# Rotary embedding: moving the cos table's load from ScalarE's queue to SyncE's, behind the first piece of x

## The chip, the cores and the metric

One core of one Trainium2 chip. The metric is the device time of one execution in microseconds (us); lower is better. The engines are called TensorE (PE in the profile, PEld for its weight loads), VectorE (DVE), ScalarE (ACT), GpSimd (POOL) and SyncE (SP). SyncE computes nothing here; it issues DMAs.

## The reference

```python
# x: (16, 512, 1024) float32; cos, sin: (512, 32) float32; num_heads = 16
x = x.reshape(batch, seq, num_heads, head_dim)           # head_dim 64, half_dim 32
x1, x2 = x[..., :half_dim], x[..., half_dim:]
cos = cos[None, :, None, :]; sin = sin[None, :, None, :]
rotated = np.concatenate([x1 * cos - x2 * sin, x1 * sin + x2 * cos], axis=-1)
```

33.55 MB come in and 33.55 MB go out. The two tables are 64 KB each.

## The kernel before

x is cut into eight tiles of 4 MB (128 partitions, 8 rows of 1,024 elements on each). There are places for five tiles; a result overwrites its input and is stored from there. Everything that moves x is issued by SyncE, in a fixed order: five tiles in, stores 0, 1 and 2, load 5, load 6 and 7 together, and the remaining stores.

```python
FIRST = (3, 8)                       # tile 0 comes as rows 0-2, then rows 3-7
# ... (pools, helpers)
tabs = bp.tile([P, 2 * dim], FP32, name="b")
sin_sb = tabs[:PB, : KK * half]                      # 64 partitions x 256
cos_sb = tabs[:PB, dim : dim + KK * half]
nc.scalar.dma_start(out=sin_sb, in_=sin_v)
nc.scalar.dma_start(out=cos_sb, in_=cos_v)
for _ in range(2):
    nc.sync.nop(hint="pause")
load(0, 0, FIRST[0])
for lo, hi in zip(FIRST, FIRST[1:]):
    load(0, lo, hi)
load(1)
load(2)
load_two(3)
# ... (identity, zeroed PSUM)
nc.tensor.matmul(out=sin_t, lhsT=spread, rhs=sin_sb, start=True, stop=True)   # 64 -> 128 partitions
nc.tensor.matmul(out=cos_t, lhsT=spread, rhs=cos_sb, start=True, stop=True)
# ... (sin_k: a view of sin_t)
nc.vector.tensor_scalar_mul(out=sns[:, :, 0, :], in0=sin_k, scalar1=-1.0)     # GpSimd's table
nc.vector.tensor_copy(out=sns[:, :, 1, :], in_=sin_k)
# ... (own_t: a part of the PSUM tile of cos)
nc.vector.tensor_copy(out=own_t, in_=sns[:, ROW_OWN])
# ... (helpers)
def stores(t):
    if t == 4:
        store_two(3)
    elif t != 3:
        store(t)
    if t == 2:
        load(5)
        load_two(6)
```

Per tile GpSimd multiplies x (halves swapped) by sin into a buffer `b`. VectorE multiplies x by cos into PSUM and adds the two (`pair_sum`, the line L199). TensorE adds for the remaining rows, and ScalarE copies those out. So GpSimd needs sin, and VectorE needs cos for its first product and GpSimd's `b` for each sum.

## Time and profile before

| | before |
|---|---|
| time, median of 6 runs | 162.32 us (162.24 to 162.7) |
| span of the profiled run | 160.7 us |
| VectorE busy | 136.3 us (85%) |
| GpSimd busy | 127.1 us (79%) |
| moved by DMA | 67.25 MB, mean 419 GB/s |
| sin, cos: issue to landing | 6.5 us, 9.3 us |
| last store: issue, landing | 148.2 us, 159.8 us |

Two things are to be read apart. A busy share tells how full an engine is on average. A DMA "lands" when the last of its sixteen completion signals, one for each DMA engine, has arrived. The landing of the last store is what ends the program. The prediction shows the lines.

### The profile page before, as it was taken

What the parts mean: (1) busy time and instruction counts of PE and PEld (TensorE: products, weight loads), DVE (VectorE), ACT (ScalarE), POOL (GpSimd) and SP (SyncE); (2) the same over time, 40 slices, a digit from 0 to 9 for tenths busy, and PEclk for the clock granted to TensorE, in tenths of its full rate; (3) what the DMA queues carried; (4) which work ended last, traced back from release to release, by engine and by line L of the source; (5) the groups of instructions that cost most, each with busy time, mean ns of one, the idle gap of its engine ahead of it and who ended that gap; (6) DMA issues with size and microseconds to landing.
All of it is one profiled execution on the core that took longest, in us unless ns stands there. A gap on an engine that the chain in (4) does not pass through costs nothing.

```text
span 160.7 us, 433 instructions
## 1 busy us (share of the span) xinstructions
PE 57.2 (36%) x71; PEld 18.8 (12%) x71; DVE 136.3 (85%) x85; ACT 18.0 (11%) x25; POOL 127.1 (79%) x38
## 2 busy tenths in 40 slices
PE   3140825055503731191309250645047402922000
PEld 0110301021102210121003010211022101310000
DVE  1029999999999999999999999999999999998000
ACT  0000331003000301021100310031003010201000
POOL 1069999999999889988998899892999999960000
PEclk9999995558555765567555955585557655675555
DMA  5999999999999999999999999999999999999993
GB/s 168 411 431 458 408 473 424 392 449 465 392 449 449 408 392 506 408 392 498 410 400 465 441 400 441 465 392 432 473 400 416 489 400 416 473 408 408 392 506 147
DMA packets 2562, 67.25 MB, mean 419 GB/s; under 512 B 257, under 2 KB 385, under 8 KB 385
## 3 DMA queue, kind: packets, MB, share of 16 engines
q1 hardware_dynamic: 2400, 67.11, 97.6%
q10 hardware_dynamic: 160, 0.13, 0.2%
q14 instruction: 2, 0.01, 0.0%
HBM read 33.69 MB, written 33.55 MB: 418 GB/s over the span
## 4 chain that ended last, share of the span: by engine, by line
DVE 74%; issue 11%; DMA 6%; PE 1%; ACTq 0%; DVEq 0%
DVE x L199 34%; DVE pd L151 33%; DMA b<-in_cos_dram 6%; DVE pe_ps L151 5%; DVE own_ps L151 1%; PE tab L124 1%; ACTq L91 0%; DVE x L160 0%; DVE tab L129 0%; DVEq L199 0%
## 5 line engine op out<-in xcount | busy, mean ns | idle before, releaser
L175 POOL TENSOR_TENSOR b<-x,sns 128x2048 f32<-128x2048 f32 (+1 forms) x32 | 126.4, 3983 | 15.4 <-DVE sns L127 8.1
L199 DVE TENSOR_TENSOR x<-pd,b 128x2048 f32<-128x2048 f32 x24 | 54.9, 2288 | 0.9
L151 DVE TENSOR_TENSOR pd<-x,tab 128x2048 f32<-128x2048 f32 x24 | 55.0, 2292 | 0.2
L186 PE MATMUL own_ps<-x,ident 128*128 128x512 f32 x32 | 29.6, 1082 | 53.3 <-DVE x L160 48.3
L186 PE MATMUL pe_ps<-b,ident 128*128 128x512 f32 x32 | 25.1, 877 | 27.2 <-DVE pe_ps L151 27.2
L186 PEld LDWEIGHTS own_ps<-x,ident 128*128 128x128 f32 x32 | 9.4, 324 | 73.2 <-DVE x L160 59.3
L219 ACT COPY x<-own_ps 128x1024 f32<-128x1024 f32 x8 | 8.1, 1013 | 72.8 <-PE own_ps L186 72.8
L191 ACT COPY x<-pe_ps 128x512 f32<-128x512 f32 x16 | 9.4, 589 | 38.7 <-PE pe_ps L186 38.7
L186 PEld LDWEIGHTS pe_ps<-b,ident 128*128 128x128 f32 x32 | 8.2, 286 | 42.2 <-DVE pe_ps L151 33.9
L151 DVE TENSOR_TENSOR pe_ps<-x,tab 128x512 f32<-128x512 f32 x16 | 11.0, 687 | 0.0
L151 DVE TENSOR_TENSOR own_ps<-x,tab 128x1024 f32<-128x1024 f32 x8 | 9.8, 1224 | 0.0
L160 DVE TENSOR_TENSOR x<-x,tab 128x1024 f32<-128x1024 f32 x8 | 9.7, 1214 | 0.0
L126 DVE TENSOR_SCALAR sns<-pd 128x256 f32<-128x256 f32 x1 | 0.4, 425 | 7.0 <-PE pd L123 7.0
L219 ACT ACT_TABLE_LOAD x1 | 1.3, 1283 | 16.8 <-DVE x L160 16.8
L123 PE MATMUL pd<-b,spread 64*128 64x256 f32 x2 | 1.2, 696 | 4.7 <-DMA b<-in_sin_dram 4.7
L129 DVE COPY tab<-sns 128x64 f32<-128x64 f32 x1 | 0.2, 228 | 2.6 <-PE tab L124 2.6
L124 PE MATMUL tab<-b,spread 64*128 64x256 f32 x2 | 1.2, 708 | 2.1 <-DMA b<-in_cos_dram 2.1
L111 PE MATMUL own_ps<-zero 128*128 128x512 bf16 x2 | 1.0, 622 | 1.2 <-DVE zero L107 1.2
L123 PEld LDWEIGHTS pd<-b,spread 64*128 64x128 f32 x2 | 0.5, 306 | 5.6 <-issue 5.6
L107 DVE MEMSET zero<- 128x256 uint32 x1 | 0.3, 272 | 0.9 <-PEq L250 0.9
L124 PEld LDWEIGHTS tab<-b,spread 64*128 64x128 f32 x2 | 0.5, 310 | 2.9 <-DMA b<-in_cos_dram 2.9
L111 PE MATMUL pe_ps<-zero 128*128 128x512 bf16 x1 | 0.6, 634 | 0.0
(9 smaller groups left out, 1.8 us busy)
## 6 DMA issues: line engine op xcount, KB each, us to landing
out_dram<-x SPq DMA_DIRECT2D x6, 4096.0 KB, 21.4
x<-in_x_dram SPq DMA_DIRECT2D x2, 8192.0 KB, 39.5
x<-in_x_dram SPq DMA_DIRECT2D x3, 4096.0 KB, 27.2
out_dram<-x SPq DMA_DIRECT2D x1, 8192.0 KB, 32.6
x<-in_x_dram SPq DMA_DIRECT2D x1, 2560.0 KB, 12.4
x<-in_x_dram SPq DMA_DIRECT2D x1, 1536.0 KB, 6.6
b<-in_sin_dram ACTq DMA_DIRECT2D x1, 64.0 KB, 6.5
b<-in_cos_dram ACTq DMA_DIRECT2D x1, 64.0 KB, 9.3
```

Source lines behind the costliest of these rows:

```text
L107: nc.vector.memset(zero, 0.0)
L111: nc.tensor.matmul(out=ps, lhsT=zero[:, :P], rhs=zero, start=True, stop=True)
L123: nc.tensor.matmul(out=sin_t, lhsT=spread, rhs=sin_sb, start=True, stop=True)
L124: nc.tensor.matmul(out=cos_t, lhsT=spread, rhs=cos_sb, start=True, stop=True)
L126: nc.vector.tensor_scalar_mul(out=sns[:, :, 0, :], in0=sin_k, scalar1=-1.0)
L151: nc.vector.tensor_tensor(out=o, in0=i, in1=cb, op=ALU.mult)
L160: nc.vector.tensor_tensor(out=heads(r), in0=heads(r), in1=s, op=ALU.mult)
L175: nc.gpsimd.tensor_tensor(out=o, in0=i, in1=sb, op=ALU.mult)
L186: nc.tensor.matmul(out=ps, lhsT=ident, rhs=other, start=False, stop=True, skip_group_check=True)
L191: nc.scalar.copy(out=r, in_=pe_ps)
L199: nc.vector.tensor_tensor(out=r, in0=ps, in1=b, op=ALU.add)
L219: nc.scalar.copy(out=r0, in_=own_ps)
```

## The change

The intent: let VectorE start earlier by bringing cos sooner. cos now stands on SyncE's queue, right behind the first piece of x, instead of behind sin on ScalarE's queue. The two no-ops that held SyncE back go.

```diff
     nc.scalar.dma_start(out=sin_sb, in_=sin_v)
-    nc.scalar.dma_start(out=cos_sb, in_=cos_v)
-    for _ in range(2):
-        nc.sync.nop(hint="pause")
     load(0, 0, FIRST[0])
+    nc.sync.dma_start(out=cos_sb, in_=cos_v)
     for lo, hi in zip(FIRST, FIRST[1:]):
         load(0, lo, hi)
```

Two lines fewer: L199 of the kernel before is L197 of the changed one, L151 is L149, L175 is L173.

## The prediction

> **What bounds the kernel now.** I read the page first, for busy shares and for the forty slices of DMA.
>
> ```profile
> span 160.7 us, 433 instructions
> PE 57.2 (36%) x71; PEld 18.8 (12%) x71; DVE 136.3 (85%) x85; ACT 18.0 (11%) x25; POOL 127.1 (79%) x38
> ...
> DMA 5999999999999999999999999999999999999993
> ...
> DMA packets 2562, 67.25 MB, mean 419 GB/s; under 512 B 257, under 2 KB 385, under 8 KB 385
> ```
>
> DVE at 85% looks like the bound, but the DMA row has a 9 in every slice except the first and the last, and 67.25 MB has to move. Second, the chain of waits, in order of time, over the first 20 us:
>
> ```profile
> 0.73 0.54 ACTq L91
> ...
> 1.30 9.32 DMA b<-in_cos_dram
> ...
> 10.66 1.23 PE tab L124 x2
> ...
> 11.92 0.24 DVE tab L129
> ...
> 12.18 1.23 DVE own_ps L151
> ```
>
> This is what the change aims at: the 64 KB of cos take 9.32 us from issue to landing, and VectorE's first product (L151) stands behind them until 12.18 us. From there the chain is nearly all VectorE. But it ends with VectorE's last sum at 148.15 us, 12.5 us before the span's end, because the last store is no engine's busy work. So, third, stretches (engine columns, then granted clock, DMA share, GB/s):
>
> ```profile
> 2.00:4.00 2.00, 0.65 (x2) 0.00 (x0) 0.00 (x0) 0.00 (x0) 0.00 (x0) 1.00 0.83 289
> ...
> 16.00:148.00 132.00, 53.30 (x64) 17.56 (x64) 130.82 (x78) 18.01 (x25) 119.83 (x31) 0.62 1.00 433
> 148.00:158.00 10.00, 0.00 (x0) 0.00 (x0) 0.15 (x1) 0.00 (x0) 0.00 (x0) 0.50 0.99 423
> 158.00:160.70 2.70, 0.00 (x0) 0.00 (x0) 0.00 (x0) 0.00 (x0) 0.00 (x0) 0.50 0.03 12
> ```
>
> From 16 to 148 us VectorE and DMA are both full (130.82 of 132 us, and a share of 1.00), so busy shares alone do not decide. What decides is whether a queue stands in front of the DMA engines when a store is issued. Fourth, the last three stores, one at a time (issue line, then time from issue to landing):
>
> ```profile
> L83 SPq DMA_DIRECT2D out_dram<-x x1: 357/357/357, 115.2 to 115.2; - x1
> ...
> DMA to landing us min/median/max: 25.3/25.3/25.3
> ```
> ```profile
> L83 SPq DMA_DIRECT2D out_dram<-x x1: 344/344/344, 132.2 to 132.2; - x1
> ...
> DMA to landing us min/median/max: 18.0/18.0/18.0
> ```
> ```profile
> L83 SPq DMA_DIRECT2D out_dram<-x x1: 332/332/332, 148.2 to 148.2; - x1
> ...
> DMA to landing us min/median/max: 11.6/11.6/11.6
> ```
>
> They land at 115.2 + 25.3 = 140.5, 132.2 + 18.0 = 150.2 and 148.2 + 11.6 = 159.8 us: 9.7 us apart, though they are issued 16 to 17 us apart. 4,194,304 bytes in 9.7 us is 432 GB/s, the rate of the whole middle. The queue of waiting bytes shrinks (25.3, 18.0, 11.6) but is not empty at the last one: an idle path would need about 1.0 us from issue to first packet (0.83 to 1.83 us for the first x piece, in the packet records), 9.7 us of data and 0.3 us from the last packet (159.52) to the landing (159.84), 11.0 us together. So some 0.6 us of work still stood ahead of the last store. **DMA sets the end**, and VectorE misses being the bound by only about 0.6 us.
>
> **What the Trainium skill says.** "DMA: Bandwidth & Descriptors", section "Issuing engines are not separate DMA queues": DMAs of SyncE, ScalarE and GpSimd run on the same 16 engines and interleave. The trace agrees: queue 1 (x and out) and queue 10 (tables) are served in turn from 4.15 to 10.2 us. Same page, "Queues, rings and completion order": each engine goes round-robin over its rings, packet by packet. The trace shows it one row at a time: a 1,024-byte table row (0.046 us) after each x row, of 12,288 bytes (0.46 us) or 20,480 bytes (0.82 us). "Perfetto Trace Analysis", section "Roofline": one active core is bounded by its 16 DMA engines, about 435 GB/s in total. The trace agrees with 433. Same page, "DMA Instruction — HWDGE (DVE, Sync)": the profiled window of an issue leaves out the data movement. So an SP issue of 0.4 us must not be read as a transfer, and I use landings.
>
> **The change, part by part.**
>
> 1. Two no-ops off SyncE. Its records show them at 0.721 and 0.767, with the first x issue at 0.828. Removed, that issue starts near 0.72, **0.11 us earlier**. Nothing is ahead of it, so the first packet (1.83 us) moves with it, and with it all the traffic behind it. This lies on the path.
>
> 2. cos off ScalarE's queue. 64 rows over 16 engines are 4 rows on each, for either table. sin goes first on queue 10 and takes the turns beside the 12 KB rows; cos gets its turns beside the 20 KB rows of the second piece, which is why it lands at 1.30 + 9.32 = 10.62 against sin's 7.21 (0.73 + 6.5). Each cos row stretches an engine's cycle from about 0.767 us (20 KB alone) to 0.854 us, 0.087 for a row whose own record is 0.046. Behind the first piece on SyncE's queue, the 4 rows should cost 4 x 0.046 = 0.18 us instead of 4 x 0.087 = 0.35. **0.16 us of DMA time saved**, on the path; this half rests on my reading of packet spacing and could be zero.
>
> 3. cos lands early. The first piece lands at 0.83 + 6.6 = 7.4 us now; with 0.11 off and 0.18 for the cos rows I estimate 7.5, three microseconds earlier. sin still lands near 7.2 and its two matmul passes run from 7.35 to 8.54; cos follows on TensorE at about 8.57 instead of 10.66. Matmul start to first product was 12.18 - 10.66 = 1.52 us, so the first product starts near **10.1 us, 2.1 us earlier**. GpSimd waits for sin alone (start 9.41) and does not move.
>
> 4. One more issue on SyncE (about 0.5 us) delays the second piece's issue from 1.27 to about 1.7 us, while the engines are busy with the first piece until 6.6: hidden.
>
> What is part 3 worth at the end? The stores come 2.1 us earlier into a queue that is already full. Their order is fixed in the program, all on SyncE's queue, and no byte disappears. It even gets lost before: the load of tiles 6 and 7 is issued at 82.4 us and takes 29.1, landing at 111.44, and VectorE starts tile 6 with almost no slack:
>
> ```profile
> 111.58 6.83 POOL L175 TENSOR_TENSOR b<-x,sns 128x2048 f32<-128x2048 f32 x2 [3.16 <-DMA x<-in_x_dram]
> 111.71 1.23 DVE L151 TENSOR_TENSOR own_ps<-x,tab 128x1024 f32<-128x1024 f32 x1
> ```
>
> VectorE would be ready at about 109.6 and would stand until 111.2 or so. So its 2.1 us are swallowed there, and its last sum still ends near 148. Part 3 adds **0** to the total. Sum: 0.11 + 0.16 = 0.27 us. 162.38 - 0.27 = **162.1 us**.
>
> **The rivals.**
>
> *VectorE is the bound, and the head start reaches the end:* 162.38 - 2.1 = 160.2 us. For it: 85% busy, and the chain of waits. Against it: the three landings 9.7 us apart, and the wait at 111.4 us, which ends with a transfer. 4 in 100.
>
> *The tables come later or disturb the start:* without the no-ops the first x issue goes out with or before sin, and sin's rows could wait behind more 12 KB rows, 0.46 us each; on the shared descriptor path ScalarE's issue could be held by SyncE's 0.38 us. GpSimd and VectorE would start up to 1 us later than I think. But against 12.18 today there is room, so the end hardly notices. It would cost only the 0.27 us: 162.4.
>
> *The transfers are merely reordered:* part 2 saves nothing, and only the no-ops count: 162.3 us. This lies well within the range.
>
> *A deeper pull into VectorE:* it now runs closer behind GpSimd. The slack at the first sum falls from 16.65 - 13.38 = 3.3 us (GpSimd's first product ends near 13.4) to about 1.1; at the second sum to a few tenths. Here part of the 2.1 us can turn into a wait on GpSimd, but VectorE would have to end over 0.6 us later than now to move the end.
>
> **Range and chances.** The three timed runs before lie at 162.28 to 162.7. My candidates lie at 162.1 (chosen), 162.3 to 162.4 (if a small term fails) and 160.2 (the first rival). With that spread and a tenth or two for the clock of the runs, 8 in 10 is 161.6 to 162.6. 2% is 3.2 us, more than even the first rival gives: faster 0.01, slower 0.01, same 0.98.
>
> **What would show it.** Right: cos lands near 7.5 us and the first product starts near 10.1; the last stores still land 9.7 us apart, with the time to landing of those before the tile 6 load grown by about 2 us; the idle time of VectorE before tile 6's first product grows to between 1 and 2 us, ended by the transfer of x; the last sum ends near 148 and the last landing is 0.1 to 0.4 us earlier. Wrong: the last store issued 2 us earlier and landing 2 us earlier (DMA was not the bound); a share of DMA that falls in a middle slice (a gap I don't expect); or sin landing after 8.5 us, so that the order of the tables costs what it should give.

## The result, and the profile after

| | before | changed |
|---|---|---|
| time, median of 6 runs | 162.32 us (162.24 to 162.7) | 162.46 us (162.14 to 162.74) |
| first x packet | 1.83 us | 1.74 us |
| sin landed / cos landed | 7.21 / 10.62 us | 7.71 / 7.91 us |
| GpSimd's first product | 9.41 us | 9.91 us |
| VectorE's first product | 12.18 us | 10.20 us |
| VectorE's second sum of tile 0 | 21.84 us | 21.26 us |
| last store issued | 148.23 us | 147.96 us |
| last store landed | 159.84 us | 159.73 us |

The ratio is 1.0003, 95% interval 0.9987 to 1.0019. Nothing measurable came of it, though VectorE's first product comes 1.98 us earlier.

The table's lower rows show where most of the 1.98 us went, in three steps. Here is the changed kernel in order of time (start, duration, engine, line, operation; in brackets the idle time before and what ended it):

```profile
9.91 22.57 POOL L173 TENSOR_TENSOR b<-x,sns 128x2048 f32<-128x2048 f32 x6 [8.60 <-DVE sns L125]
...
10.20 1.23 DVE L149 TENSOR_TENSOR own_ps<-x,tab 128x1024 f32<-128x1024 f32 x1
...
21.26 2.29 DVE L197 TENSOR_TENSOR x<-pd,b 128x2048 f32<-128x2048 f32 x1 [1.51 <-POOL b L173]
```
```profile
111.44 1.23 DVE L149 TENSOR_TENSOR own_ps<-x,tab 128x1024 f32<-128x1024 f32 x1 [0.22 <-DMA x<-in_x_dram]
111.48 6.83 POOL L173 TENSOR_TENSOR b<-x,sns 128x2048 f32<-128x2048 f32 x2 [3.65 <-DMA x<-in_x_dram]
```

And the lines of the kernel before that answer to the second sum and to the last store:

```profile
21.84 2.29 DVE L199 TENSOR_TENSOR x<-pd,b 128x2048 f32<-128x2048 f32 x1
```
```profile
148.23 0.33 SPq L83 DMA_DIRECT2D out_dram<-x  x1
```

First, VectorE waits 1.51 us for GpSimd at its second sum, a wait that the kernel before has not. GpSimd itself starts 0.50 us later than before, because sin lands 0.50 us later. But that is the smaller part. In the kernel before, GpSimd's product for this sum ended at 20.71 us by its own record (the next one began at 20.66), 1.13 us before VectorE's sum began. A head start of 1.98 us uses these up and runs 0.85 us ahead of GpSimd even with sin on time. Of 1.98 us, 21.84 - 21.26 = 0.58 are left, so 1.40 us are lost here.

Second, VectorE runs into the load of tiles 6 and 7 at 111.44 us; after it 111.71 - 111.44 = 0.27 us are left, which is what the last store's issue shows. The chain that ended last, followed back, now passes through two transfers here, the store of tile 2 and the load into the place that it frees; in the kernel before it stays on VectorE from 12.18 us on:

```profile
63.70 18.49 DMA out_dram<-x
...
82.27 29.08 DMA x<-in_x_dram
...
111.44 0.06 DVE own_ps L149
```

Third, the stores of the changed kernel wait in the same queue. The last three again, issue and time to landing:

```profile
L83 SPq DMA_DIRECT2D out_dram<-x x1: 357/357/357, 114.9 to 114.9; - x1
...
DMA to landing us min/median/max: 25.4/25.4/25.4
```
```profile
L83 SPq DMA_DIRECT2D out_dram<-x x1: 344/344/344, 131.9 to 131.9; - x1
...
DMA to landing us min/median/max: 18.2/18.2/18.2
```
```profile
L83 SPq DMA_DIRECT2D out_dram<-x x1: 333/333/333, 148.0 to 148.0; - x1
...
DMA to landing us min/median/max: 11.8/11.8/11.8
```

They land at 140.4, 150.1 and 159.7 us, 9.7 us apart as before. Issued 0.27 us earlier, the last one takes 0.16 us longer (11.77 against 11.61), and 0.11 us are left at the landing. The rate in the middle of the program is unchanged, too (same columns as in the prediction's table of stretches; the third number from the end is the granted clock, then DMA share and GB/s):

```profile
16.00:148.00 132.00, 51.58 (x64) 16.72 (x62) 129.08 (x77) 16.89 (x25) 120.26 (x31) 0.62 1.00 433
148.00:158.00 10.00, 0.00 (x0) 0.00 (x0) 0.00 (x0) 0.00 (x0) 0.00 (x0) 0.50 0.98 423
```

VectorE's 129.08 instead of 130.82 us says that it now waits 1.7 us in this stretch, between the same two ends. DMA stays at a share of 1.00 and 433 GB/s.

### The profile page after: what moved, and what is told of

Read it like the earlier page. It is cut to its first block, busy times and chain, and to the rows that moved or that the text cites. A ratio compares the mean times of both kernels' runs of the same rounds, so it can differ in the third digit from the quotient of the medians.

```text
span 160.6 us, 431 instructions
## 1 busy us (share of the span) xinstructions
PE 56.2 (35%) x71; PEld 18.8 (12%) x71; DVE 136.4 (85%) x85; ACT 18.1 (11%) x25; POOL 127.1 (79%) x38
## 4 chain that ended last, share of the span: by engine, by line
DVE 43%; DMA 34%; issue 7%; POOL 7%; PE 1%; DVEq 0%; SPq 0%
DVE x L197 21%; DVE pd L149 18%; DMA x<-in_x_dram 18%; DMA out_dram<-x 12%; POOL b L173 7%; DMA b<-in_sin_dram 4%; DVE pe_ps L149 2%; PE pd L121 1%; DVE sns L124 0%; DVE sns L125 0%; DVE own_ps L149 0%; DVE x L158 0%; DVEq L197 0%; SPq L80 0%; SPq L83 0%
## 5 line engine op out<-in xcount | busy, mean ns | idle before, releaser
L173 POOL TENSOR_TENSOR b<-x,sns 128x2048 f32<-128x2048 f32 (+1 forms) x32 | 126.4, 3989 | 15.4 <-DVE sns L125 8.6
L197 DVE TENSOR_TENSOR x<-pd,b 128x2048 f32<-128x2048 f32 x24 | 54.9, 2287 | 2.3 <-POOL b L173 1.5
L149 DVE TENSOR_TENSOR pd<-x,tab 128x2048 f32<-128x2048 f32 x24 | 55.0, 2292 | 0.2
L184 PE MATMUL own_ps<-x,ident 128*128 128x512 f32 x32 | 28.9, 1059 | 53.6 <-DVE x L158 48.6
L149 DVE TENSOR_TENSOR pe_ps<-x,tab 128x512 f32<-128x512 f32 x16 | 11.0, 686 | 0.0
L149 DVE TENSOR_TENSOR own_ps<-x,tab 128x1024 f32<-128x1024 f32 x8 | 9.8, 1224 | 0.3 <-DMA x<-in_x_dram 0.2
```

Source lines behind the costliest of these rows:

```text
L149: nc.vector.tensor_tensor(out=o, in0=i, in1=cb, op=ALU.mult)
L173: nc.gpsimd.tensor_tensor(out=o, in0=i, in1=sb, op=ALU.mult)
L184: nc.tensor.matmul(out=ps, lhsT=ident, rhs=other, start=False, stop=True, skip_group_check=True)
L197: nc.vector.tensor_tensor(out=r, in0=ps, in1=b, op=ALU.add)
```

## The experiments

The theory: the transfers set the end, and an earlier VectorE only lengthens their queue. The main rival: VectorE sets the end, and its head start was lost for a reason of its own. Ten kernels ran, in three sets, each compared with the kernel before of its own rounds: the three relieved kernels and cos ahead of the first piece (162.41 us); cos late, the two halves of the change and the delayed second piece (162.35 us); the 24 no-ops and both tables on SyncE (162.46 us).

### Relieving the DMA engines

Both kernels lose 8 MB of traffic, so no queue is left before the last store. Their outputs are wrong, which doesn't matter for the times.

```diff
     if t == 2:
         load(5)
-        load_two(6)
```

On the kernel before:

> The kernel before without the load of tiles 6 and 7 (8 MB; their places keep old data, so the result is wrong on purpose). Theory (DMA sets the end, by about 0.6 us): nothing queues before the last store, so it takes about 11.0 us from issue to landing instead of 11.6, and VectorE's wait of 0.2 us before tile 6 goes: about 161.4 us, 0.9 below before, VectorE's last sum at about 147.9 us. Rival (VectorE sets the end): only the 0.2 us go, 162.1 us.

On the changed kernel:

> The changed kernel without the load of tiles 6 and 7 (wrong result on purpose). Theory: with DMA off the end, what is left of VectorE's head start after its wait for GpSimd in tile 0 (0.58 us) shows at last: about 160.8 us, 0.6 below the relieved kernel before, although the full kernels are alike. Rival (the head start of 0.58 us is worthless for another reason, for example lost again in GpSimd's buffers): equal to the relieved kernel before.

Measured: 162.53 us for the relieved kernel before, 161.51 us for the relieved changed kernel: 1.02 us between medians, where the full kernels differ by nothing. In the traces the last store is issued at 148.36 and 147.58 us, 0.78 apart, and needs 11.1 us in both:

```profile
L83 SPq DMA_DIRECT2D out_dram<-x x1: 332/332/332, 148.4 to 148.4; - x1
...
DMA to landing us min/median/max: 11.1/11.1/11.1
```
```profile
L83 SPq DMA_DIRECT2D out_dram<-x x1: 332/332/332, 147.6 to 147.6; - x1
...
DMA to landing us min/median/max: 11.1/11.1/11.1
```

So what is left of the head start after the wait for GpSimd is real, and it reaches the end once the transfers are out of the way: the 0.78 us stand already at the second sum (21.98 and 21.20 us). Both expectations failed in their absolute values (161.4 and 160.8 us). For the first, 0.9 us below before was expected, and the relieved kernel before was not faster at all. Part of that is plain. The last store went from 11.61 to 11.08 us, 0.53 off, not 0.6. The 0.2 us "wait" ahead of tile 6 never existed (below). In the profiled run VectorE's first product came at 12.32 instead of 12.18 us, which this kernel, unlike the full one, pays in full. And its timed runs lie about 2.1 us above their spans, against 1.8 us for the kernel before (162.42 for a span of 160.3; 162.41 for 160.6). Why that part outside the span grew is open, so the two relieved kernels are compared with each other only.

With the two no-ops put back on SyncE into the second of these kernels:

> The changed kernel with the two no-ops back on SyncE, without the load of tiles 6 and 7 (wrong result on purpose). Theory (the no-ops let sin go ahead and GpSimd start at 9.4 instead of 9.9 us, and GpSimd caps VectorE's head start): 0.5 us below the changed kernel relieved, about 160.3 us. Rival (the order of issues doesn't matter to sin): equal to it, 160.8 us.

161.62 us, not 160.3. sin landed at 7.59 us and GpSimd started at 9.79: the no-ops don't bring sin back. The expectation was wrong, and the rival was right that this kernel equals the one without the no-ops; the later experiments with no-ops take this up.

### Early costs nothing, late costs

cos behind the second piece of tile 0:

```diff
     load(0, 0, FIRST[0])
-    nc.sync.dma_start(out=cos_sb, in_=cos_v)
     for lo, hi in zip(FIRST, FIRST[1:]):
         load(0, lo, hi)
+    nc.sync.dma_start(out=cos_sb, in_=cos_v)
     load(1)
```

> cos issued by SyncE behind the second piece of the first tile. Theory: cos lands near 13.9 us, VectorE's first product comes near 15.5, 3.3 us later than before; less the slack of 0.2 us before tile 6 and of 0.6 us at the last store the end moves by 2.5 us: about 164.9 us. Late costs what early didn't gain. Rival (VectorE sets the end without slack): 165.7 us. Rival (DMA has much more slack than I read): under 163.5 us.

165.18 us, ratio 1.0171 (1.0158 to 1.0184). VectorE's first product came 3.39 us later than in the kernel before, its last store was issued 3.38 us later (151.61) and landed 2.85 us later (162.69):

```profile
15.57 1.23 DVE L149 TENSOR_TENSOR own_ps<-x,tab 128x1024 f32<-128x1024 f32 x1
```
```profile
L83 SPq DMA_DIRECT2D out_dram<-x x1: 332/332/332, 151.6 to 151.6; - x1
...
DMA to landing us min/median/max: 11.1/11.1/11.1
```

An empty path takes 11.08 us, so the queue before the last store was 11.61 - 11.08 = 0.53 us in the kernel before. The time rose by 165.18 - 162.35 = 2.83 us, which is 3.38 less 0.53. 3.39 at the first product became 3.38 at the last store: VectorE had no slack before tile 6, and the 0.2 us that this expectation took off there were none.

This is the shape of a bound with two nearly equal sides. VectorE has to be 0.53 us late before the end feels it. By being early it gained nothing in the times (0.11 us at the last landing of the trace).

### Delaying the transfers while VectorE starts early

The changed kernel with 24 no-ops ahead of the first x issue:

```diff
+    for _ in range(24):
+        nc.sync.nop(hint="pause")
     load(0, 0, FIRST[0])
```

> The changed kernel with 24 no-ops on SyncE ahead of the first x issue, so that all x traffic starts about 1.1 us later (24 x 0.046 us), near 2.8 us, while sin goes ahead alone. VectorE's first product comes near 11.2 us, still 1 us earlier than in the kernel before. Theory (the bytes set the end): the end moves by the full 1.0 to 1.1 us, to about 163.4 us, although VectorE starts earlier than before. Rival (VectorE or GpSimd sets the end): 162.4 us or less.

163.0 us, ratio 1.0035 (1.0020 to 1.0050): slower, although VectorE starts 2.4 us earlier than in the kernel before:

```profile
9.82 1.23 DVE L151 TENSOR_TENSOR own_ps<-x,tab 128x1024 f32<-128x1024 f32 x1
```

GpSimd, too, starts earlier than before (8.08 against 9.41 us), and VectorE's second sum is still 0.62 us ahead (21.22 us). So neither engine can be what made it slower; the later transfers did. The load of tiles 6 and 7 landed at 112.27 us instead of 111.44, and VectorE stood for it:

```profile
112.36 1.23 DVE L151 TENSOR_TENSOR own_ps<-x,tab 128x1024 f32<-128x1024 f32 x1 [1.18 <-DMA x<-in_x_dram]
```

The size was missed: 0.54 us instead of 1.0. The first x packet came at 2.62 us, 0.88 later than in the changed kernel, but tile 0 had landed only 0.53 us later (14.29 against 13.76). The first piece took no less time without sin beside it (12 KB rows from 2.62 to 7.41 us; 1.74 to 6.51 in the changed kernel). Most of what was regained lies behind it: the first 20 KB row after cos took 0.89 us instead of 1.16, of which more below.

The profiled run is one of the two slowest of six (163.32 and 163.33; the others 162.94 to 163.01). In it the last landing is 0.93 us later than in the changed kernel, because another 0.44 us came near 51 us, at the slow turn that the next experiment shows.

cos ahead of the first piece instead:

```diff
+    nc.sync.dma_start(out=cos_sb, in_=cos_v)
     load(0, 0, FIRST[0])
-    nc.sync.dma_start(out=cos_sb, in_=cos_v)
```

> cos issued by SyncE ahead of the first piece, not behind it. Theory (DMA sets the end): VectorE's first product comes near 8.3 us, 4 us earlier than before, but the first x packet comes about 0.5 us later (near 2.3 us), so the total is 162.7 to 162.9 us, slightly slower than the changed kernel. Rival (VectorE sets the end): a start 2 us earlier than the changed kernel's, about 160.5 us.

163.34 us, ratio 1.0059 (1.0042 to 1.0077). VectorE started at 7.78 us, 4.4 us earlier than before, and the kernel is slower by 0.9 us. GpSimd, which waited for the second piece of x, took 3.3 us of these back at the second sum, but 1.11 us were left (20.73 against 21.84 us), and they went at tile 6:

```profile
20.73 2.29 DVE L197 TENSOR_TENSOR x<-pd,b 128x2048 f32<-128x2048 f32 x1 [3.25 <-POOL b L173]
...
112.48 1.23 DVE L149 TENSOR_TENSOR own_ps<-x,tab 128x1024 f32<-128x1024 f32 x1 [1.79 <-DMA x<-in_x_dram]
```

That decides against the rival as far as the end goes: an engine that was ahead had to wait for the transfers. Of the 1.98 us of the change, however, the rival explains the larger part, the 1.40 us lost to GpSimd. The cause of the size is not the one expected: tiles 0 to 2 landed as early as in the changed kernel (33.22 against 33.20 us), but tile 4 landed at 53.18 instead of 52.62. These 0.56 us are half of the 1.03 by which the last landing is later; the rest came in small steps up to the load of tiles 6 and 7. Near 50.7 us, where the loads end and the first store follows, rows of 32 KB took 1.6 to 2.0 us on all sixteen engines, instead of 1.22. What makes that turn dearer here is open.

### The two halves of the change, each alone

The kernel before without its no-ops:

> The kernel before without the two no-ops, and nothing else. Theory: x's first packet near 1.74 us, sin lands near 7.7 us, GpSimd starts near 9.9, cos still lands near 10.6 us and VectorE's first product stays near 12.2; time 162.3 us, within 0.2 of before. Rival: sin stays at 7.2 us.

163.11 us, ratio 1.0046 (1.0029 to 1.0063): slower, where the same time had been expected. The packet records show why. With the no-ops, a DMA engine moves about four 12 KB rows of x before the first row of sin gets a turn; without them, about six. Of the eight x rows of the first piece only two are then left to alternate with. sin lands at 7.90 us, and cos takes all its turns beside 20 KB rows and lands at 12.10 instead of 10.62:

```profile
13.66 1.23 DVE L149 TENSOR_TENSOR own_ps<-x,tab 128x1024 f32<-128x1024 f32 x1
```

13.66 - 12.18 = 1.48 us late, less the 0.53 us of slack, gives 0.95; the last landing of the profiled run moved from 159.84 to 160.78, by 0.94. (The timed runs fall into two groups, 162.74 to 162.79 and 163.43 to 163.46; the profiled one, with a span of 161.6 us, belongs to the upper. What chooses the group is open.)

The changed kernel with the no-ops back, that is, the move of cos alone:

> The changed kernel with the two no-ops back on SyncE. Theory: x's first packet at 1.83 us again, sin lands at 7.2 instead of 7.7 us, GpSimd starts at 9.4 instead of 9.9, VectorE's wait for GpSimd at its second sum shrinks from 1.5 to about 1.0 us; the time stays at 162.4 us within 0.2. Rival (sin's delay comes from cos on SyncE's queue): sin stays at 7.7 us.

162.5 us, ratio 1.0009 (0.9998 to 1.0021). The first sin row comes after about four x rows again, yet sin lands at 7.62 us, not 7.2, as the rival had it (sin's delay comes from cos on SyncE's queue). So the no-ops decide when sin's turns begin, but in the changed kernel they no longer decide when it lands.

Together: taking the no-ops out alone costs 0.76 us, moving cos alone costs nothing measurable, and both together cost nothing. The no-ops brought both tables forward (without them sin came 0.69 and cos 1.48 us later), but what the end felt was cos; once cos is off ScalarE's queue, taking them out costs nothing measurable.

### Where the DMA engines lost what they had gained

In the changed kernel the first 20 KB row on each engine took 1.16 us (median of the sixteen), undisturbed ones 0.77. Is it the short cos rows ahead of it in the same queue, or the later issue of the second piece? Here cos stays on ScalarE's queue, and no-ops delay the second piece's issue:

```diff
-    for _ in range(2):
-        nc.sync.nop(hint="pause")
     load(0, 0, FIRST[0])
+    for _ in range(11):
+        nc.sync.nop(hint="pause")
```

> The kernel before with no no-ops ahead of the first piece and eleven between the first and the second piece on SyncE: the second piece is issued as late as in the changed kernel (1.7 us), but cos stays on ScalarE's queue. In the changed kernel the first 20 KB packet on each DMA engine behind cos took 1.15 us instead of 0.77. Theory (the short cos rows in the same queue leave the next read uncovered): here no packet of the second piece takes over 0.95 us. Rival (the later issue does it): 1.15 us here too.

The second piece was issued at 1.58 us (1.74 in the changed kernel, 1.27 before), and its first rows took 0.80 us, none over 0.81. So the late issue does not seem to be it; the last 0.16 us were not tried. (One run, state unknown, 163.32 us, near the upper group without no-ops ahead of the first piece.) With cos behind the second piece, in the experiment on late cos, it was the first 32 KB rows that were long: 1.48 instead of 1.22 us. The long row follows the cos rows. Its length is open: with 24 no-ops, cos stood in the same place, but sin had long landed, and the first 20 KB rows took only 0.89 us.

Both tables on SyncE's queue behind the first piece:

```diff
-    nc.scalar.dma_start(out=sin_sb, in_=sin_v)
     load(0, 0, FIRST[0])
+    nc.sync.dma_start(out=sin_sb, in_=sin_v)
     nc.sync.dma_start(out=cos_sb, in_=cos_v)
```

> sin and cos both issued by SyncE behind the first piece, nothing on ScalarE's queue. Theory (short rows in x's own queue leave the next long read uncovered, and a landing near that gap is told late): no row of the first piece is interleaved, the first 20 KB row on each engine takes 1.1 us or more (0.77 undisturbed), sin lands near 7.4 us and cos near 7.9, VectorE's first product near 10.2, and the time stays within 0.3 us of 162.4. Rival (the gap comes from two queues meeting at the end of the first piece): the first 20 KB rows take under 0.9 us here, and the time falls by 0.2 us or so.

162.53 us, ratio 1.0002 (0.9986 to 1.0017). The first 20 KB rows took 1.03 us (median; 1.13 at most), so the gap does not need two queues meeting, though they may add to it. sin landed at 7.41 us, cos at 7.73, and the first product came at 9.89 us. The last landing, 159.54 us, is the earliest of the full kernels, but the times do not show it. No full version is faster than the kernel before.

## Why the prediction was right or wrong

**The total** (162.1 us, 161.6 to 162.6, "same"): measured 162.46 us, in the range, and the same as before. The reason given for the end is the one the experiments show: the transfers set it. VectorE earlier by 4.4 us at its first product and 1.11 us at its second sum did not help, the transfers later by 0.5 to 0.9 us did harm, and a head start counted when 8 MB were taken away. But of the 1.98 us, GpSimd took 1.40, the load of tiles 6 and 7 0.32 and the last store's queue 0.15; the prediction had given nearly all of it to that load.

**The queue before the last store** (about 0.6 us): 0.53 us by six kernels whose last store met an empty path (11.07 to 11.08 us). The sum was right by luck: the parts of the idle path are 0.83, 9.91 and 0.35 us in the relieved kernel before, not 1.0, 9.7 and 0.3.

**Part 1, the no-ops** (0.11 us earlier): the first x packet moved from 1.83 to 1.74 us, 0.09.

**Part 2, cos behind the first piece saves 0.16 us of DMA time**: this term failed, and its sign was wrong. Cos behind the first piece cost 0.17 us instead. The 20 KB rows of the second piece took 101.59 us before and 104.30 us after, summed over 16 engines: 0.17 us more on each. The interleaving did go, but each engine lost 0.39 us (1.16 - 0.77) on the first long row behind the short ones. Tile 0, whose first packet came 0.09 us earlier, had landed 0.08 us later (13.76 against 13.68). That is why 162.1 was a little low: nothing of the 0.27 us was left when tile 0 had landed. The last landing does come 0.11 us earlier, but that is not this gain. The lead appears only between 33 and 62 us (tile 2 0.09 us late, the first store 0.06 early), around the turn from loads to stores, where the kernel before had six rows of 1.5 us or more and the changed one none over 1.32. In the times nothing shows.

**Part 3, cos and the first product** (7.5 and 10.1 us): 7.91 and 10.20. "sin still lands near 7.2" failed: 7.71. Its last row ended at 6.60 us against 6.20 before, since the second rival's picture, sin behind more 12 KB rows, did come true: about six rows instead of four. The last of the packets that signal its completion was not late (6.64 against 6.71 us), because the rows and packets around it were short. But from that packet to the landing it took 1.1 us instead of 0.5. This happened just at the gap after the cos rows; with the no-ops back, where that packet came at 6.92 us, it took 0.7. That the gap causes the wait is argued, not shown: in both kernels three transfers complete within a few tenths of a microsecond there (the first piece, sin, cos), which is a rival that no run separates. ScalarE's issue of sin was not held by SyncE's (0.53 us against 0.54).

**Part 4, one more issue on SyncE** (1.7 us for the second piece, hidden): 1.74 us. With the second piece issued late, at 1.58 us, and cos elsewhere, its rows were not long (0.80 us).

**Where the head start is swallowed** (VectorE idle 1 to 2 us before tile 6, ended by x): this step failed. Only 0.22 us were idle there, ended by x; 1.51 us had gone to GpSimd at the second sum of tile 0. The prediction's fourth rival named that place but mis-sized it, "to a few tenths" of slack left. It let GpSimd's first product end at 13.38 us; the record ends at 13.91 (4.50 us; 13.38 fits the 3.98 us of the profile's page, which are a mean over products of two rows and of one). At the second sum the slack was 1.13 us, and 2.1 us off that is a wait of 1.0, without any delay of sin. Sin's 0.50 us made it 1.5. The growth of "about 2 us" in the time to landing of the stores before the load of tile 6 failed with it: it was 0.5 us (store 2 from 18.0 to 18.5).

**The slack before tile 6** ("almost no slack"; 0.2 us in two of the expectations): VectorE did not wait there at all. A late cos moved the first product by 3.39 and the last store by 3.38 us. The 0.22 us that the full chain of waits calls "issue" before 111.71 us lie where two products overlap on VectorE, and are no wait. The transfer, though, was 0.27 us ahead of VectorE there (111.44 against 111.71 us).

## What to carry to other kernels

When an engine and the DMA engines are both full, look at the last transfers: if their time to landing exceeds what an idle path takes, as 11.61 us against 11.08 here, a queue stands before them, and in this kernel an earlier engine made it longer. Follow a head start step by step, too: most of this one was gone at another engine 10 us after it began. Test the bound from both sides, once with the engine earlier and once with it later; here early gave 0 and late cost 2.83 us for 3.38. And a no-op that looks like dust can order two queues: taking it out alone cost 0.76 us.

## What the Trainium skill lacked or had wrong

- "DMA: Bandwidth & Descriptors", "Queues, rings and completion order", says that an engine drains a packet of some 9 to 17 descriptors before it switches rings. Here, in the packet records, it switched after every row, of 1,024 bytes or of 12 or 20 KB, while both rings had rows. The page does not say how long a new ring waits for its first turn: about four 12 KB rows with two no-ops ahead of x, about six without them.
- No page has the gap after short rows in the same ring: the first 20 KB row behind four 1 KB rows took 1.16 us instead of 0.77 (0.89 in the kernel with 24 no-ops), and the first 32 KB row 1.48 instead of 1.22.
- The same page, "Anatomy of one DMA — SWDGE (gpsimd) path", puts a fixed cost near 2.0 us on a DMA that GpSimd issues. It has no such sum for one that SyncE issues. For a 4 MB store of SyncE on an empty path 11.08 us were measured; packets moved for 9.91 of them, so 1.2 us are left.
- No page has the slow turn from loads to stores: near 50 us a 32 KB row took up to 2.0 us instead of 1.22 with cos ahead of the first piece, up to 1.7 with 24 no-ops, and hardly more than 1.3 in the changed kernel.
